# The first norm's squares taken from the transposed tiles of x, added by GpSimd and summed over partitions by TensorE

## The chip, the cores and the metric

The kernel runs on one core of a Trainium2 chip. The metric is the device time of one execution in microseconds, as the median of several runs. The engines are named as in the profile: PE (TensorE; PEld are its weight loads), DVE (VectorE), ACT (ScalarE), POOL (GpSimd) and SP (SyncE, which issues most DMA transfers). Each engine works through its own instructions in order; between engines, semaphores make an instruction wait.

## The reference

A trunk of two layers on x of 256 rows and 2048 columns, in float32. The change touches only the norm of the first layer and the projection that follows it:

```python
def rms_norm(x, g):
    xf = x.astype(jnp.float32)
    y = xf * lax.rsqrt(jnp.mean(xf * xf, axis=-1, keepdims=True) + EPS)
    return (y * g.astype(jnp.float32)).astype(x.dtype)

def gmlp_branch(xn, w_in, v_g, w_s, b_s, w_out):
    proj = xn @ w_in                              # [u | v | gate], each 4096 wide
    uv = jax.nn.gelu(proj[..., :2 * GMLP_WIDTH])
    zg = proj[..., 2 * GMLP_WIDTH:]
    u, v = jnp.split(uv, 2, axis=-1)
    v = rms_norm(v, v_g)
    ...

h = x
h = h + gmlp_branch(rms_norm(h, norm_g[0]), ...)
h = h + stick_breaking_branch(rms_norm(h, norm_g[1]), ...)
return rms_norm(h, final_g)
```

The norm's factor of a row of x, the reciprocal root of its mean square, is the same for all columns of the row. The kernel therefore multiplies x (times the gain) with the weights first, and applies the factor when it takes the products out of PSUM.

## The kernel before

All matmuls are done in float32 precision from two parts: an operand is rounded to a high part (`hi`, by ScalarE) and the rest is its low part (`lo`, by VectorE); a product is the sum of hi by hi, hi by lo and lo by hi, three matmuls of 128x512 each (`terms`). `cut` makes the parts of a tile of weights: a cast on ScalarE (L115), then a subtraction on VectorE (L116). `split_x` does the same for one contraction tile of x (128 columns of x, transposed: 128 partitions by 256 rows), with the gain: L479 on ScalarE, L480 on VectorE.

The first product is v's first two blocks of 512 columns, `v0`. Its first half of the contraction (tiles k = 0 to 7) runs over both blocks at once: for each k, 12 matmuls into four PSUM banks, with the weights `v_0` to `v_7` (`v_k_raw`, `v_k_hi`, `v_k_lo`) of 128x1024. The second half goes by columns: `v_08`, `v_010`, `v_012`, `v_014` hold two contraction tiles each of the first block, `v_18` and so on those of the second. The transposed x comes in `first` (tile 0) and `xr` (four tiles each), loaded by `load_x`. Beside this, x comes a second time, by rows: `load_h` loads four tiles `h` of 512 KB, and ScalarE squares each in two instructions with an accumulated sum (`square`, L474). `rstd` adds the sums (VectorE), and POOL raises the mean to the power -1/2 (`n_r`, L98). `evac_v` (L484) uses it.

From block 2 on, products of two blocks are computed with a Strassen-like scheme (`Pair`), which needs sums and differences of the parts of x: `left.sums` adds hi and lo (`s_full`), takes four differences (`s_sm`) and splits them again (`xs`). Before, these temporaries and the `h` tiles stand in buffers (tags `b11_1`, `b12_1`, `b21_1`, `b22_1`) that later hold weights `v_b` of the next pair; `v_p` are the parts of those weights.

The program's text doesn't fix the order in which engines get their work. A scheduler orders the instructions when the program is built, by its own model of their durations; `issue_after` and the order of the loads are bounds that it keeps. Weights' raw tiles rotate through four buffers, their parts through five. All loads of this stretch go through SP's queue in one order.

Of the kernel before, what the change touches and what calls it, by code (L numbers as in the profile page):

```python
# [29 lines left out]
def trunk_kernel(ctx: ExitStack, tc: tile.TileContext, x, xt, gcols, wst, wv0, a_w_in, a_v_norm_g,  # L30
# [19 lines left out]
    KD = D // P  # L50
    NC = D // CB
# [5 lines left out]
    const = ctx.enter_context(tc.tile_pool(name="const", bufs=1))  # L57
# [31 lines left out]
    def f(ap):  # L89
        return ap.bitcast(F32)  # L90

    def rstd(idx, nparts, n, name):
        tot = const.tile([P, NT], F32, name=f"{name}_tot")
        nc.vector.tensor_reduce(tot, ssq[:, :, idx, 0:nparts], axis=mybir.AxisListType.X, op=ALU.add)
        ms = const.tile([P, NT], F32, name=f"{name}_ms")
        nc.vector.tensor_scalar(ms, tot, 1.0 / n, EPS, op0=ALU.mult, op1=ALU.add)
        r = const.tile([P, NT], F32, name=f"{name}_r")
        nc.gpsimd.tensor_tensor(r, ms, half, op=ALU.pow)  # L98
        return r
# [7 lines left out]
    low = [None]  # L107
# [16 lines left out]
    class Left:  # L124
# [7 lines left out]
            sl = slice(t * P, (t + 1) * P)  # L132
            return self.hi[:, k, sl], self.lo[:, k, sl]

        def sums(self, ks, out, name):

            for k0 in range(0, ks, 4):
                n = min(4, ks - k0)
                full = []
                for i in range(2):  # L140
                    sl = slice(i * ks + k0, i * ks + k0 + n)
                    fl = sraw.tile([P, 4, S], F32, tag=f"b1{i + 1}_1", name=f"{name}_full{i}{k0}")
                    nc.vector.tensor_add(fl[:, 0:n], f(self.hi[:, sl, :]), f(self.lo[:, sl, :]))
                    full.append(fl)
                a11, a12 = full[0][:, 0:n, 0:P], full[1][:, 0:n, 0:P]
                a21, a22 = full[0][:, 0:n, P:S], full[1][:, 0:n, P:S]
                sm = [sraw.tile([P, 2, 4, P], F32, tag=f"b2{i + 1}_1", name=f"{name}_sm{i}{k0}") for i in range(2)]
                s1, s2, s3, s4 = sm[0][:, 0, 0:n], sm[0][:, 1, 0:n], sm[1][:, 0, 0:n], sm[1][:, 1, 0:n]
                nc.vector.tensor_sub(s1, a21, a22)
                nc.vector.tensor_sub(s3, a21, a11)  # L150
                nc.vector.tensor_sub(s2, a11, s1)
                nc.vector.tensor_sub(s4, a12, s2)
                for i, si in enumerate((s1, s2, s3, s4)):
                    o = out[:, :, i, k0:k0 + n]
                    nc.scalar.copy(o[:, 0], si)
                    nc.vector.tensor_sub(o[:, 1], si, f(o[:, 0]))
            self.s, self.ks = [out], ks
# [59 lines left out]
    def ins_of(x):  # L217
        return x.ins if hasattr(x, "ins") else x
# [219 lines left out]
    def home(tag, shape, dtype, name):  # L438
        return big.tile(shape, dtype, tag=tag, name=name)
# [4 lines left out]
    left = Left(x_hi, x_lo)  # L444
    vs_ = [home(f"v{i}", [P, NT, W // 2], F32, f"v{i}") for i in range(2)]

    def v_of(t, c0, n):

        i, c = divmod(c0, W // 2)
        return vs_[i][:, t, c:c + n]  # L450
    XC = 4
    raws = ("b11_0", "b12_0", "b22_0", "b21_0")
    xr = []

    def load_x(i):

        xr.append(sraw.tile([P, XC, S], F32, tag=raws[i], name=f"xr{i}"))
        if i > 0:
            load(xr[i], xt[:, i * XC:(i + 1) * XC, :])

    def x_of(k):
        return first[:, 0:S] if k == 0 else xr[k // XC][:, k % XC, :]

    hc = []

    def load_h(c):

# [14 lines left out]
    def evac_v(b, t, bank):  # L482
# [732 lines left out]
```

## Time and profile before

| | |
|---|---|
| median of 3 runs | 1142.49 us (1142.46 to 1146.1) |
| profiled execution: time, span | 1142.97 us, 1141.3 us |
| clock granted to TensorE | 0.999 of full speed |
| busy: PE, DVE, ACT, POOL | 1131.7, 1014.7, 832.5, 86.9 us |
| read from device memory, mean rate | 259.55 MB, 231 GB/s |

The span is from the first to the last instruction of the profiled execution, and its time includes what lies around it. Busy times are sums over the span. A matmul's end is modelled in this profile and overlaps the next, so the row's step from start to start (0.23 us for 128x512) says more than its duration.

### The profile page before, as it was taken

The page shows a single profiled execution, that of the slowest core. Times are in us where ns is not written, and L with a number is a line of the kernel's source. Part 1 is how long each engine was busy: PE and PEld are TensorE (multiplying, and loading weights), DVE is VectorE, ACT ScalarE, POOL GpSimd, SP SyncE. Part 2 cuts the span into 40 slices and gives each one's busy share as a digit, 9 for nine tenths or more (in the row PEclk, how much of TensorE's full clock was granted, in tenths as well). Part 3 has the DMA queues.
Part 4 walks back from the last instruction along what each step waited for, and adds up shares of the span by engine and source line. Part 5 has one row for each costly group of instructions (what it writes and reads, how often), then busy time and mean ns, then how long its engine had stood idle before and what let it go on. Part 6 is the DMA issues. An engine that isn't in the chain of part 4 may idle for free.

```text
span 1141.3 us, 14869 instructions
## 1 busy us (share of the span) xinstructions
PE 1131.7 (99%) x5169; PEld 937.7 (82%) x5169; DVE 1014.7 (89%) x1114; ACT 832.5 (73%) x1104; POOL 86.9 (8%) x106
## 2 busy tenths in 40 slices
PE   9999999999999999999999999999999999999997
PEld 6878888888888888888888888888888888888886
DVE  7999899999999999978989779889889989897986
ACT  7777678777777778766657457688678887886564
POOL 0210110110110110000010001100100101000000
PEclk9999999999999999999999999999999999999999
DMA  9997787687687687585785867687687776838951
GB/s 353 325 319 243 219 268 255 186 270 260 162 266 266 181 259 258 152 301 140 268 237 185 325 188 257 174 242 221 178 279 205 201 240 178 256 99 275 337 181 74
DMA packets 79227, 264.72 MB, mean 232 GB/s; under 512 B 9008, under 2 KB 9520, under 8 KB 79024
## 3 DMA queue, kind: packets, MB, share of 16 engines
q1 hardware_dynamic: 67472, 228.10, 57.0%
q0 software_dynamic: 10672, 33.04, 15.9%
q10 hardware_dynamic: 1008, 2.65, 0.6%
q8 instruction: 40, 0.66, 0.2%
q14 instruction: 35, 0.29, 0.1%
HBM read 259.55 MB, written 4.19 MB: 231 GB/s over the span
## 4 chain that ended last, share of the span: by engine, by line
PE 93%; DMA 3%; ACT 1%; DVE 1%; issue 1%; SPq 0%; DVEq 0%; POOLq 0%; POOL 0%; ACTq 0%
PE gu_a L120 3%; PE gu_b L120 3%; PE gu_a L121 3%; PE gu_b L121 3%; PE gu_b L122 3%; PE gu_a L122 3%; PE op_acc L122 2%; PE op_acc L120 2%; PE op_acc L121 2%; DMA v_raw<-in_a_w_in 2%; PE gu_d L120 2%; PE gu_d L121 2%; PE gu_c L120 2%; PE gu_c L122 2%; PE gu_d L122 2%; PE gu_c L121 2%
## 5 line engine op out<-in xcount | busy, mean ns | idle before, releaser
L115 ACT CAST gu_p_hi<-gu_b 128x1024 fp32r<-128x1024 f32 (+1 forms) x126 | 123.5, 1006 | 52.7 <-PE gu_c L122 17.7
L116 DVE TENSOR_TENSOR gu_p_lo<-gu_b,gu_p_hi 128x1024 fp32r<-128x1024 f32 (+1 forms) x126 | 143.5, 1164 | 10.0 <-ACT gu_p_hi L115 8.7
L116 DVE TENSOR_TENSOR qk_p_lo<-qk_b,qk_p_hi 128x1024 fp32r<-128x1024 f32 (+1 forms) x77 | 80.7, 1074 | 13.9 <-ACT qk_p_hi L115 13.3
L115 ACT CAST qk_p_hi<-qk_b 128x1024 fp32r<-128x1024 f32 (+1 forms) x77 | 70.5, 934 | 27.1 <-PE o_c L122 7.7
L115 ACT CAST gu_hi<-gu_raw 128x1024 fp32r<-128x1024 f32 x60 | 61.8, 1054 | 19.7 <-PE gu_d L122 13.5
L116 DVE TENSOR_TENSOR gu_lo<-gu_raw,gu_hi 128x1024 fp32r<-128x1024 f32 x60 | 71.4, 1216 | 4.8 <-ACT gu_hi L115 4.7
L116 DVE TENSOR_TENSOR v_p_lo<-v_b,v_p_hi 128x1024 fp32r<-128x1024 f32 x42 | 50.2, 1221 | 7.4 <-ACT v_p_hi L115 7.1
L115 ACT CAST v_hi<-v_raw 128x1024 fp32r<-128x1024 f32 (+1 forms) x43 | 41.9, 989 | 20.4 <-DMA v_raw<-in_a_w_in 9.8
L116 DVE TENSOR_TENSOR v_lo<-v_raw,v_hi 128x1024 fp32r<-128x1024 f32 (+1 forms) x43 | 49.1, 1146 | 7.2 <-ACT v_hi L115 6.8
L115 ACT CAST v_p_hi<-v_b 128x1024 fp32r<-128x1024 f32 x42 | 43.0, 1050 | 12.4 <-PE v_c L122 6.3
L116 DVE TENSOR_TENSOR bv_p_lo<-bv_b,bv_p_hi 128x1024 fp32r<-128x1024 f32 (+1 forms) x42 | 42.7, 1041 | 7.4 <-ACT bv_p_hi L115 7.1
L115 ACT CAST o_p_hi<-o_b 128x1024 fp32r<-128x1024 f32 (+1 forms) x35 | 33.4, 965 | 19.3 <-PE op_acc L122 13.8
L116 DVE TENSOR_TENSOR bg_p_lo<-bg_b,bg_p_hi 128x1024 fp32r<-128x1024 f32 (+1 forms) x42 | 42.5, 1042 | 5.0 <-ACT bg_p_hi L115 5.0
L115 ACT CAST bv_p_hi<-bv_b 128x1024 fp32r<-128x1024 f32 (+1 forms) x42 | 37.6, 908 | 12.8 <-PE qk_c L122 5.2
L115 ACT CAST bg_p_hi<-bg_b 128x1024 fp32r<-128x1024 f32 (+1 forms) x42 | 37.2, 906 | 9.4 <-PE bg_a L122 2.5
L116 DVE TENSOR_TENSOR o_p_lo<-o_b,o_p_hi 128x1024 fp32r<-128x1024 f32 (+1 forms) x35 | 38.2, 1113 | 5.3 <-ACT o_p_hi L115 5.3
L287 DVE TENSOR_TENSOR gu_b<-gu_b,gu_b 128x1024 f32<-128x1024 f32 (+1 forms) x36 | 41.5, 1165 | 1.1 <-DMA gu_b<-in_a_w_in 0.8
L115 ACT CAST op_hi<-op_raw 128x1024 fp32r<-128x1024 f32 x24 | 25.2, 1053 | 19.6 <-PE op_acc L122 10.8
L121 PE MATMUL op_acc<-op_lo,yc 128*128 128x512 f32 x96 | 37.7, 392 | 0.0
L122 PE MATMUL op_acc<-op_hi,yc 128*128 128x512 f32 x96 | 37.6, 394 | 0.0
L115 ACT CAST o_hi<-o_raw 128x1024 fp32r<-128x1024 f32 x22 | 23.0, 1055 | 19.9 <-PE o_d L122 10.2
L295 POOL DMA_DIRECT2D gu_b<-in_a_w_in x20 | 17.5, 874 | 251.0 <-DMA gu_raw<-in_a_w_in 79.5
(807 smaller groups left out, 3778.8 us busy)
## 6 DMA issues: line engine op xcount, KB each, us to landing
gu_b<-in_a_w_in SPq DMA_DIRECT2D x64, 512.0 KB, 4.9
gu_raw<-in_a_w_in SPq DMA_DIRECT2D x60, 512.0 KB, 5.2
v_raw<-in_a_w_in SPq DMA_DIRECT2D x32, 512.0 KB, 5.7
qk_b<-in_b_w_in SPq DMA_DIRECT2D x32, 512.0 KB, 4.7
qk_raw<-in_b_w_in SPq DMA_DIRECT2D x26, 512.0 KB, 5.2
v_b<-in_a_w_in SPq DMA_DIRECT2D x24, 512.0 KB, 5.1
op_raw<-in_a_w_out SPq DMA_DIRECT2D x24, 512.0 KB, 4.5
o_raw<-in_a_w_out SPq DMA_DIRECT2D x22, 512.0 KB, 4.7
```

The lines of the kernel that those rows point to most:

```text
L115: nc.scalar.copy(hi[:, sl], raw[:, sl])
L116: low[0] = nc.vector.tensor_sub(lo[:, sl], raw[:, sl], f(hi[:, sl]))
L120: nc.tensor.matmul(acc, lh, hi, start=first, stop=False, skip_group_check=True)
L121: nc.tensor.matmul(acc, lh, lo, start=False, stop=False, skip_group_check=True)
L122: nc.tensor.matmul(acc, ll, hi, start=False, stop=last, skip_group_check=True)
L287: nc.vector.tensor_sub(into[g], b0[g], b1[g])
L295: adds.append(nc.gpsimd.dma_start(into[g], self.src(HALVES[i][k], n, j), accum_op=ALU.add))
```

## The change

Each of the four groups of four contraction tiles of x (one of `first` and three of `xr0`, then `xr1`, `xr2`, `xr3`) is squared by ScalarE in whole (`square`), into a part of the tiles `vs_`, which are free that early (`slot`). POOL adds the four tiles of a group to one and that to a running total (`fold`: one add of 128x512 and one or two of 128x256). `rstd_x` splits the total into a high part (ScalarE) and a low part (VectorE), and four matmuls with a vector of ones sum over the partitions; then the mean and the power -1/2 follow as before. The four loads of x by rows and their squares are gone. `left.sums` gets its temporaries in `vs_` as well and is called earlier, bound to come after the low part of `v_08`. A power on POOL that nothing uses (`early`) is put at the start.

```diff
+    early = const.tile([P, NT], F32, name="early")
+    nc.gpsimd.tensor_tensor(early, nc.const_aps.tensor(1.0, [P, NT], F32), half, op=ALU.pow)
...
-        def sums(self, ks, out, name):
+        def sums(self, ks, out, name, at=None):
...
-                    fl = sraw.tile([P, 4, S], F32, tag=f"b1{i + 1}_1", name=f"{name}_full{i}{k0}")
+                    fl = sraw.tile([P, 4, S], F32, tag=f"b1{i + 1}_1", name=f"{name}_full{i}{k0}") if at is None else \
+                        at[i].rearrange("p (k s) -> p k s", k=4)
...
-    def load_h(c):
-        hc.append(sraw.tile([P, NT, CB], F32, tag=("b11_1", "b12_1", "b21_1", "b22_1")[c], name=f"h0_{c}"))
-        load(hc[c], x[c])
+    total = jk.tile([P, 2, S], F32, tag="sg0", bufs=1, name="total")
...
     def square(i):
-        c, t = divmod(i, NT)
-        junk = jk.tile([P, CB], BF16, tag="junk", bufs=1, name=f"junk0_{c}_{t}")
-        nc.scalar.activation(junk, hc[c][:, t, :], AF.Square, accum_out=ssq[:, t, 0, c:c + 1])
+        sq = slot(i).rearrange("p (k s) -> p k s", k=XC)
+        sqs.append(sq)
+        if i == 0:
+            nc.scalar.activation(sq[:, 0, :], first[:, 0:S], AF.Square)
+            nc.scalar.activation(sq[:, 1:XC, :], xr[0][:, 1:XC, :], AF.Square)
+        else:
+            nc.scalar.activation(sq, xr[i], AF.Square)
+
+    def fold(i):
+        sq = sqs[i]
+        nc.gpsimd.tensor_add(sq[:, 0:2], sq[:, 0:2], sq[:, 2:4])
+        nc.gpsimd.tensor_add(total[:, min(i, 1)], sq[:, 0], sq[:, 1])
+        if i > 0:
+            nc.gpsimd.tensor_add(total[:, 0], total[:, 0], total[:, 1])
+
+    def rstd_x():
+        parts = jk.tile([P, 2, S], F32R, tag="sg1", bufs=1, name="parts")
+        nc.scalar.copy(parts[:, 0], total[:, 0])
+        nc.vector.tensor_sub(parts[:, 1], total[:, 0], f(parts[:, 0]))
+        ones = const.tile([P, 2], F32R, name="ones_r")
+        nc.scalar.activation(ones, half, AF.Identity, scale=-2.0)
+        tot = ps_ms.tile([P, NT, 2], F32, tag="ms", name="n0_tot")
+        for t in range(NT):
+            for i in range(2):
+                nc.tensor.matmul(tot[:, t], parts[:, i, t * P:(t + 1) * P], ones, start=i == 0, stop=i == 1)
+        ms = const.tile([P, NT], F32, name="n0_ms")
+        nc.vector.tensor_scalar(ms, tot[:, :, 0], 1.0 / D, EPS, op0=ALU.mult, op1=ALU.add)
+        r = const.tile([P, NT], F32, name="n0_r")
+        nc.gpsimd.tensor_tensor(r, ms, half, op=ALU.pow)
+        return r
...
-    beyond = {3: lambda: load_x(1), 4: lambda: load_x(2), 5: lambda: load_h(0), 6: lambda: load_x(3),
-              7: lambda: load_h(1)}
+    beyond = {3: lambda: load_x(1), 4: lambda: load_x(2), 6: lambda: load_x(3)}
...
-        if k >= 6:
-            square(k - 6)
+        if k in (4, 6, 7, 9):
+            square((4, 6, 7, 9).index(k))
+        if k in (4, 6, 7, 9):
+            fold((4, 6, 7, 9).index(k))
...
-            r1 = rstd(0, NC, D, "n0")
+            r1 = rstd_x()
         next(col)
-        if i < 2:
-            load_h(2 + i)
-        if i < 3:
-            square(2 + 2 * i)
-            square(3 + 2 * i)
-    left.sums(KS_A, home("xs", [P, 2, 4, KS_A, P], F32R, "xs0"), "s0")
+        if i == 0:
+            with tc.issue_after(ins_of(low[0])):
+                left.sums(KS_A, home("xs", [P, 2, 4, KS_A, P], F32R, "xs0"), "s0",
+                          [slot(i) for i in (4, 5, 0, 1)])
+        if KD // 2 + i in (4, 6, 7, 9):
+            square((4, 6, 7, 9).index(KD // 2 + i))
+        if KD // 2 + i in (4, 6, 7, 9):
+            fold((4, 6, 7, 9).index(KD // 2 + i))
```

The scheduler puts the new work among the old as follows; behind the first pair of blocks the order of every engine is the same as before. Numbers in names are the program's own.

On ScalarE, before, from the scaling of x's tile 3 to the cast of `v_6` (`xr_195` and `xr_217` hold x's tiles 4 to 7 and 8 to 11, `h_0` rows of x):

```order
L479 ACTIVATE x_hi<-xr_122,cols 128x256
L115 CAST v_3_hi<-v_3_raw 128x1024
L479 ACTIVATE x_hi<-xr_195,cols 128x256 x4
L115 CAST v_4_hi<-v_4_raw 128x1024
L479 ACTIVATE x_hi<-xr_217,cols 128x256 x4
L115 CAST v_5_hi<-v_5_raw 128x1024
L474 ACTIVATE junk_0_0_269,ssq<-h_0_239 128x512
L474 ACTIVATE junk_0_1_293,ssq<-h_0_239 128x512
L115 CAST v_6_hi<-v_6_raw 128x1024
```

On ScalarE now, the same stretch (`v_117` and `v_118` are the tiles `vs_` with the squares):

```order
L483 ACTIVATE v_117<-xr_125 128x768
L117 CAST v_3_hi<-v_3_raw 128x1024
L514 ACTIVATE x_hi<-xr_198,cols 128x256 x3
L485 ACTIVATE v_117<-xr_198 128x1024
L514 ACTIVATE x_hi<-xr_198,cols 128x256
L117 CAST v_4_hi<-v_4_raw 128x1024
L485 ACTIVATE v_118<-xr_220 128x1024
L514 ACTIVATE x_hi<-xr_220,cols 128x256 x4
L117 CAST v_5_hi<-v_5_raw 128x1024
L117 CAST v_6_hi<-v_6_raw 128x1024
```

The squares of the first three groups stand ahead of `v_3_hi`, `v_4_hi` and `v_5_hi`; before, the first square stood behind `v_5_hi`.

On VectorE, before, the products' low parts from `v_6` on and the sums (`s_full`, `s_sm`):

```order
L143 TENSOR_TENSOR s_full_430<-x_hi,x_lo 128x1024
L116 TENSOR_TENSOR v_6_lo<-v_6_raw,v_6_hi 128x1024
L480 SCALAR_TENSOR_TENSOR x_lo<-xr_261,cols,x_hi 128x256 x4
L116 TENSOR_TENSOR v_7_lo<-v_7_raw,v_7_hi 128x1024
L143 TENSOR_TENSOR s_full_432<-x_hi,x_lo 128x1024
L116 TENSOR_TENSOR v_08_lo<-v_08_raw,v_08_hi 128x1024
```

On VectorE now, from `v_6` on (`v_118<-x_hi,x_lo` are the two sums that were `s_full`):

```order
L118 TENSOR_TENSOR v_6_lo<-v_6_raw,v_6_hi 128x1024
L515 SCALAR_TENSOR_TENSOR x_lo<-xr_266,cols,x_hi 128x256 x4
L118 TENSOR_TENSOR v_7_lo<-v_7_raw,v_7_hi 128x1024
L118 TENSOR_TENSOR v_08_lo<-v_08_raw,v_08_hi 128x1024
L146 TENSOR_TENSOR v_118<-x_hi,x_lo 128x1024 x2
L118 TENSOR_TENSOR v_010_lo<-v_010_raw,v_010_hi 128x1024
L498 TENSOR_TENSOR parts<-total,parts 128x256
```

The two sums moved from ahead of `v_6_lo` and `v_08_lo` to behind `v_08_lo`, and the low part of the total follows `v_010_lo`.

On TensorE now, the first of the four matmuls over the partitions (`n_tot`) between the products of `v_08` (before, the row didn't exist and the others stood in the same order):

```order
L122 MATMUL v_acc_120<-v_08_hi,x_hi 128x512
L122 MATMUL v_acc_121<-v_08_hi,x_hi 128x512
L504 MATMUL n_tot<-ones_r,parts 128x2
L123 MATMUL v_acc_120<-v_08_lo,x_hi 128x512
L124 MATMUL v_acc_120<-v_08_hi,x_lo 128x512
L123 MATMUL v_acc_121<-v_08_lo,x_hi 128x512
```

It stands ahead of all products of `v_08` with its low part; the other three come behind the first two products of `v_012`.

More of the change, by code (lines that the diff above doesn't have):

```diff
@@ L146, in sums @@
                 a21, a22 = full[0][:, 0:n, P:S], full[1][:, 0:n, P:S]
-                sm = [sraw.tile([P, 2, 4, P], F32, tag=f"b2{i + 1}_1", name=f"{name}_sm{i}{k0}") for i in range(2)]
+                sm = [sraw.tile([P, 2, 4, P], F32, tag=f"b2{i + 1}_1", name=f"{name}_sm{i}{k0}") if at is None else
+                      at[2 + i].rearrange("p (h k s) -> p h k s", h=2, k=4) for i in range(2)]
                 s1, s2, s3, s4 = sm[0][:, 0, 0:n], sm[0][:, 1, 0:n], sm[1][:, 0, 0:n], sm[1][:, 1, 0:n]
@@ L450, in v_of, with slot @@
         return vs_[i][:, t, c:c + n]
+    def slot(i):
+        v, t, c = ((0, 0, 1), (0, 1, 1), (1, 0, 0), (1, 0, 1), (1, 1, 0), (1, 1, 1))[i]
+        n = NT * CB
+        return vs_[v][:, t, c * n:(c + 1) * n]
     XC = 4
@@ L462, in x_of @@
         return first[:, 0:S] if k == 0 else xr[k // XC][:, k % XC, :]
-    hc = []
-    def load_h(c):
-        hc.append(sraw.tile([P, NT, CB], F32, tag=("b11_1", "b12_1", "b21_1", "b22_1")[c], name=f"h0_{c}"))
-        load(hc[c], x[c])
+    total = jk.tile([P, 2, S], F32, tag="sg0", bufs=1, name="total")
+    sqs = []
     def square(i):
-        c, t = divmod(i, NT)
-        junk = jk.tile([P, CB], BF16, tag="junk", bufs=1, name=f"junk0_{c}_{t}")
-        nc.scalar.activation(junk, hc[c][:, t, :], AF.Square, accum_out=ssq[:, t, 0, c:c + 1])
+        sq = slot(i).rearrange("p (k s) -> p k s", k=XC)
[26 more added lines that the diff above has]
+        return r
     def split_x(k):
```

## The prediction

> **What bounds the kernel now.** I read the page's head first, then the list of what TensorE waited for, then the engines' busy time in the stretch that the change touches (10 to 30 us), and then that stretch instruction by instruction. In the waits the columns are total, times, longest; in the stretches, busy us (instructions) of PE, PEld, DVE, ACT and POOL, then clock, DMA share and GB/s.
>
> ```profile
> span 1141.3 us, 14869 instructions
> PE 1131.7 (99%) x5169; PEld 937.7 (82%) x5169; DVE 1014.7 (89%) x1114; ACT 832.5 (73%) x1104; POOL 86.9 (8%) x106
> ...
> PE wps L78 <- PEq L1203: 0.8, 1, 0.8
> PE v_acc L120 <- ACT v_hi L115: 0.8, 1, 0.8
> PE v_c L120 <- ACT v_c L332: 0.4, 1, 0.4
> PE gT L435 <- ACT bsg L1024: 0.2, 1, 0.2
> ...
> 10.00:15.00 5.00, 5.00 (x24) 4.08 (x23) 4.11 (x8) 4.16 (x8) 0.00 (x0) 1.00 1.03 408
> 15.00:20.00 5.00, 5.00 (x24) 4.14 (x23) 4.92 (x9) 4.97 (x12) 0.00 (x0) 1.00 1.03 415
> 20.00:25.00 5.00, 5.00 (x24) 4.14 (x23) 5.00 (x8) 4.83 (x10) 0.00 (x0) 1.00 1.02 408
> 25.00:30.00 5.00, 5.00 (x24) 4.14 (x23) 4.67 (x6) 4.81 (x11) 0.00 (x0) 1.00 1.03 407
> ```
>
> TensorE is the bound: it works in 99% of the span, and after the first matmuls its waits add up to 1.4 us in the whole run. So little is to be gained anywhere, and each microsecond by which TensorE is made to wait at the start is added to the end, since no later idle time absorbs it. From 10 to 30 us VectorE, ScalarE and the DMA engines are all full as well and TensorE just keeps its pace (clock 1.00); POOL does nothing there. The question is by how much the new work of ScalarE and POOL makes VectorE late in that stretch. The rows below are ScalarE's, VectorE's and one weight load of TensorE's (start, duration; a group xN counts as one).
>
> ```profile
> 11.62 0.51 ACT L479 ACTIVATE x_hi<-xr,cols 128x256 fp32r<-128x256 f32 x1
> 12.16 1.05 ACT L115 CAST v_hi<-v_raw 128x1024 fp32r<-128x1024 f32 x1
> 13.45 1.72 ACT L479 ACTIVATE x_hi<-xr,cols 128x256 fp32r<-128x256 f32 x4 [0.24 <-DMA xr<-in_xt]
> 15.06 1.03 ACT L115 CAST v_hi<-v_raw 128x1024 fp32r<-128x1024 f32 x1
> 16.01 1.71 ACT L479 ACTIVATE x_hi<-xr,cols 128x256 fp32r<-128x256 f32 x4
> 17.62 1.04 ACT L115 CAST v_hi<-v_raw 128x1024 fp32r<-128x1024 f32 x1
> ...
> 13.24 1.23 DVE L116 TENSOR_TENSOR v_lo<-v_raw,v_hi 128x1024 fp32r<-128x1024 f32 x1 [0.33 <-ACT v_hi L115]
> 14.38 1.67 DVE L480 SCALAR_TENSOR_TENSOR x_lo<-xr,cols,x_hi 128x256 fp32r<-128x256 f32 x4
> 16.13 1.23 DVE L116 TENSOR_TENSOR v_lo<-v_raw,v_hi 128x1024 fp32r<-128x1024 f32 x1
> 17.27 1.67 DVE L480 SCALAR_TENSOR_TENSOR x_lo<-xr,cols,x_hi 128x256 fp32r<-128x256 f32 x4
> 18.86 1.22 DVE L116 TENSOR_TENSOR v_lo<-v_raw,v_hi 128x1024 fp32r<-128x1024 f32 x1
> 20.08 1.23 DVE L143 TENSOR_TENSOR s_full<-x_hi,x_lo 128x1024 f32<-128x1024 f32 x1
> ...
> 20.88 0.19 PEld L121 LDWEIGHTS v_acc<-v_lo,x_hi 128*128 128x128 f32 x1
> 28.58 0.19 PEld L121 LDWEIGHTS v_acc<-v_lo,x_hi 128*128 128x128 f32 x1
> ```
>
> The last three L115 rows are v_3_hi, v_4_hi and v_5_hi, the L116 rows v_3_lo, v_4_lo and v_5_lo. TensorE takes up v_5_lo at 20.88, 0.8 us after it is done (18.86 + 1.22 = 20.08): that is all the room there is. From start to next start, a 128x1024 cast takes ScalarE 0.95 us (15.06 to 16.01), four 128x256 scalings 1.61 (13.45 to 15.06; 0.40 each), and VectorE needs 1.14 for a low part (13.24 to 14.38) and 1.59 for four x_lo (17.27 to 18.86).
>
> **The change, part 1: ScalarE's squares come before the casts that TensorE needs.** The change puts a 128x768 square ahead of v_3_hi and a 128x1024 square ahead of each of v_4_hi and v_5_hi; before, no square stood ahead of v_5_hi. No row has a 128x1024 square; the nearest is the cast of that size, 0.95, and I take 0.74 for 768. From 11.62: 0.40 + 0.74 + 0.95 (v_3_hi) + 1.61 + 0.95 + 0.95 (v_4_hi) + 0.95 + 1.61 = 8.16, so v_5_hi starts at 19.78 instead of 17.62 and ends at 20.82; v_5_lo ends 1.22 later, at 22.04. By ScalarE alone TensorE is 1.2 us late. Were these squares free (lower bound), 0. Of the loads, v_3 to v_5 and their x tiles stand ahead of the first removed load in SP's queue, so they come no earlier.
>
> **Part 2: POOL's adds hold VectorE up.** POOL had nothing here. Its reads are priced by the row in which POOL meets a busy VectorE:
>
> ```profile
> 253.69 1.22 DVE L116 TENSOR_TENSOR gu_lo<-gu_raw,gu_hi 128x1024 fp32r<-128x1024 f32 x1
> 254.83 1.43 DVE L315 TENSOR_TENSOR gu_b<-gu_b,gu_b 128x1024 f32<-128x1024 f32 x1
> ...
> 254.16 1.01 POOL L615 TENSOR_SCALAR_AFFINE_SELECT ws<-ws 128x256 f32<-128x256 f32 x1 [6.95 <-DMA ws<-in_wst]
> 424.85 2.76 POOL L615 TENSOR_SCALAR_AFFINE_SELECT ws<-ws 128x256 f32<-128x256 f32 x1 [4.67 <-DMA ws<-in_wst]
> L615 POOL TENSOR_SCALAR_AFFINE_SELECT ws<-ws 128x256 f32<-128x256 f32 x8 | 9.4, 1173 | 45.8 <-DMA ws<-in_wst 45.8
> ```
>
> The select starts at 254.16, while VectorE is busy; it ends at 255.17, 0.34 after VectorE's next instruction began, and that instruction takes 1.43 instead of 1.22. So POOL waits for a gap between two VectorE instructions, and its reading of 256 elements a partition then costs VectorE 0.21. An add with two inputs of 512 reads 1024, one of 256 reads 512. Folds 0 to 2 (one add of 128x512 and one of 128x256, then twice one and two) read 3 x 1024 + 5 x 512 = 22 x 256 elements: 22 x 0.21 = 4.62 us. Their squares are done by about 12.9, 15.9 and 18.2, so all of it falls ahead of the end of v_5_lo. VectorE's own way there, from v_3_lo (12.76 + 1.04, thus 13.83): 1.14 + 1.59 + 1.14 + 1.59 + 1.22 = 6.68, to 20.51; with the holds 25.13. TensorE wants it at 20.88: **4.25 us late**. ScalarE's 22.04 is inside that, so parts 1 and 2 make 4.25 together and not 5.4. Ends: if POOL holds nothing up, 1.2 (part 1); if VectorE is shut out for the whole 0.34 per 256, 22 x 0.34 = 7.5, to 28.0, thus 7.1 late. I take 0.21, since it is what the row shows for a read.
>
> [...]
>
> Behind v_5_lo the sums' two 128x1024 adds (1.14 each) now stand after v_08_lo, which frees 2.28 before it, and fold 3 takes 8 x 0.21 = 1.7 of that: nothing more. The late x loads are no help, since VectorE is the late one.
>
> **Part 3: four matmuls of 128x2.** They stand in TensorE's order between v_08's and v_012's.
>
> ```profile
> 698.45 1.03 PE L435 MATMUL hT<-ident,h 128*128 128x128 f32 x8
> 699.24 0.48 PE L120 MATMUL qk_c<-qk_p_hi,xs 128*128 128x512 f32 x1
> ...
> 60.55 0.63 ACT L486 ACTIVATE junkv<-v 128x512 bf16<-128x512 f32 x1
> 61.17 0.58 ACT L332 COPY v_c<-v_b 128x512 f32<-128x512 f32 x1
> ...
> 33.02 5.09 POOL L98 TENSOR_TENSOR n_r<-n_ms,half 128x2 f32<-128x2 f32 x1 [31.64 <-DVE n_ms L96]
> 184.40 0.73 POOL L98 TENSOR_TENSOR nv_r<-nv_ms,half 128x2 f32<-128x2 f32 x1 [9.11 <-DVE nv_ms L96]
> 39.06 1.26 ACT L484 ACTIVATE v<-v_acc,n_r 128x512 f32<-128x512 f32 x2
> ...
> 3.29 0.51 ACT L479 ACTIVATE x_hi<-first,cols 128x256 fp32r<-128x256 f32 x1 [0.54 <-DMA cols<-in_gcols]
> 4.39 1.28 ACT L115 CAST v_hi<-v_raw 128x512 fp32r<-128x512 f32 x2 [0.60 <-DMA v_raw<-in_wv]
> h<-in_x SPq DMA_DIRECT2D x8, 512.0 KB, 8.2
> ```
>
> The nearest are transposes, 0.79 / 8 = 0.1 each: **+0.4** (0 to 0.8). The first waits for ScalarE's copy of POOL's total and stands where TensorE is at 28.58 now, 32.8 when 4.25 late. POOL's last squares are ready at about 22.7 (two more casts and one square after 19.78); three adds with a wait each end near 27. Six microseconds of room: 0. If it is gone, v_08's low products and all behind them wait there.
>
> **Part 4: the rest.** The copy v_c has two squares of `junkv` ahead of it now and one in the changed order; that is 0.6 us of ScalarE, and TensorE's only wait in this stretch (0.4 at v_c) goes: **-0.4** (0 to -0.6). Nothing is late next there, as no other wait is listed. The four removed loads are 512 KB each, at 408 GB/s 1.28 us, 5.1 us of DMA time; all stand behind v_5's load, at a time when VectorE and not the DMA sets the pace, and TensorE had no wait for a load after 10 us: 0. The `early` power moves the long first one (5.09 against 0.73) to the start, where POOL is idle until 12.9, and before its end at 38.11 was covered by ScalarE's first use at 39.06: 0. The constant of ones and the first square (0.2 and 0.4) are covered by ScalarE's idle 0.54 and 0.60 at 3.29 and 4.39; without that cover they would cost 0.6. VectorE's added `parts` (0.40) and removed reduction (0.15) fall in its freed time.
>
> Sum: 4.25 + 0.4 - 0.4 = +4.25 on the profiled execution, 1142.97 us by its own time (span 1141.3 and 1.7 around it). It stands 0.5 above the median of the three runs, 1142.49, from which I count: **1146.7 us**.
>
> **The rivals.**
> 1. Not slower: POOL's adds cost VectorE nothing, or POOL alone waits. For it: the select itself waited up to 2.76 us and VectorE lost only 0.21. Then part 1 remains: 1142.5 + 1.2 = 1143.7, within what a measurement of this kernel can tell from no change (0.3%, 3.4 us). It decides where the delay is 3.4 us, v_5_lo then ending at 24.3: 3.8 us of holds, or 0.17 per 256 elements read.
> 2. Longer holds: POOL's two-input adds keep VectorE out for their whole time. For it: 0.34 from grant to end; against it: only 0.21 showed on VectorE. 7.1 + 0 = 1149.6.
> 3. POOL's chain comes too late for TensorE's n_tot. Eleven adds start at 12.9; the mean of the small selects is 1.17 with one input of 256. At 2 us each they end at 34.9, the copy at 35.4, 6.8 after 28.58: 1149.3. It decides from about 1.8 us an add when VectorE is 4.25 late.
> 4. The saved DMA time pays: 0.4 of TensorE's waits goes and the squares hide behind earlier loads: 1142.1. Against it: v_3 to v_5 aren't loaded earlier.
>
> **How the numbers follow.** The forecast (POOL's reads delay VectorE by about 0.21 per 256) has 0.50, with 1145.3 to 1148.3 as its own range; a sixth of it (0.08) lies below 1145.9, within 0.3%. Rival 1 has 0.28, rivals 2 and 3 together 0.19, rival 4 0.03. Slower by over 0.3%: 0.42 + 0.19 = 0.61; within: 0.08 + 0.28 + 0.02 = 0.38; faster by over 0.3%: 0.01, as TensorE's waits hold less than that. The range goes from rival 1 with 0.4 off (1143.3) to rival 2 (1149.7).
>
> **What would show it.** In the changed profile: v_5_lo ending near 25 instead of 20.08; VectorE's instructions between 13 and 25 us longer by 0.4 to 0.9 where a POOL add runs; a new wait of TensorE for v_4_lo and v_5_lo of about 4 us in all, none at n_tot; no wait at v_c; everything behind 90 us as before but later. Wrong if v_5_lo ends near 22 (rival 1), beyond 27 (rival 2), or if TensorE's wait stands at n_tot (rival 3).

## The result and the profile after

The changed kernel takes 1149.86 us (median of 6 runs, 1148.67 to 1150.26) against 1142.93 us for the kernel before on the same chip (6 runs, 1141.75 to 1146.1): ratio 1.0058, 95% interval 1.0047 to 1.0069, thus 6.9 us slower. The profiled execution took 1150.13 us. From here on times are those of the profile's span, and the page's head and TensorE's waits (total, times, longest) answer to the first rows shown of before:

```profile
span 1148.4 us, 14872 instructions
PE 1136.0 (99%) x5173; PEld 939.8 (82%) x5173; DVE 1021.0 (89%) x1114; ACT 831.0 (72%) x1095; POOL 101.8 (9%) x118
...
PE v_acc L123 <- DVE v_lo L118: 3.3, 2, 3.1
...
PE v_c L122 <- ACT v_c L336: 0.4, 1, 0.4
```

TensorE now waits 3.3 us for low parts that VectorE makes, where it waited for none. The 0.8 of `v_hi` at 9.59 us in the old profile is gone (v's second tile had landed 1.26 us sooner); such waits at the start differ between runs (none here, 0.5 in the run without the adds). The wait at `v_c` has stayed.

The engines' busy time in the stretch that the change touches, columns as before (PE, PEld, DVE, ACT, POOL, then clock, DMA share, GB/s):

```profile
10.00:15.00 5.00, 5.00 (x23) 3.83 (x21) 3.21 (x6) 4.70 (x9) 2.25 (x2) 1.00 1.02 414
15.00:20.00 5.00, 3.21 (x13) 2.10 (x12) 5.00 (x6) 5.00 (x9) 4.74 (x5) 1.00 0.85 342
20.00:25.00 5.00, 3.62 (x9) 2.84 (x10) 5.00 (x5) 4.95 (x8) 4.76 (x5) 0.52 0.34 107
25.00:30.00 5.00, 4.76 (x18) 3.36 (x17) 5.00 (x8) 1.05 (x1) 0.89 (x2) 0.80 0.32 111
```

From 20 to 25 us VectorE is busy throughout but finishes 5 instructions instead of 8; POOL is busy beside it. TensorE, which issued 24, issues 9, and for part of the time at half clock (0.52 on the mean). The DMA falls to a third: raw weights wait for the buffers that VectorE is late to free (SP's longest wait for a `v_lo` from 15 to 30 us is 5.9 us, before it was 2.3). Now VectorE's and POOL's instructions there (start, duration):

```profile
13.56 1.49 DVE L118 TENSOR_TENSOR v_lo<-v_raw,v_hi 128x1024 fp32r<-128x1024 f32 x1 [0.92 <-ACT v_hi L117]
14.98 4.14 DVE L515 SCALAR_TENSOR_TENSOR x_lo<-xr,cols,x_hi 128x256 fp32r<-128x256 f32 x4
19.05 2.28 DVE L118 TENSOR_TENSOR v_lo<-v_raw,v_hi 128x1024 fp32r<-128x1024 f32 x1
21.25 4.12 DVE L515 SCALAR_TENSOR_TENSOR x_lo<-xr,cols,x_hi 128x256 fp32r<-128x256 f32 x4
25.30 2.89 DVE L118 TENSOR_TENSOR v_lo<-v_raw,v_hi 128x1024 fp32r<-128x1024 f32 x2
...
12.68 1.30 POOL L489 TENSOR_TENSOR v<-v 128x512 f32<-128x512 f32 x1 [10.67 <-ACT v L483]
14.05 1.61 POOL L490 TENSOR_TENSOR total<-v 128x256 f32<-128x256 f32 x1
...
18.80 1.44 POOL L489 TENSOR_TENSOR v<-v 128x512 f32<-128x512 f32 x1
20.32 1.60 POOL L490 TENSOR_TENSOR total<-v 128x256 f32<-128x256 f32 x1
...
22.75 1.46 POOL L489 TENSOR_TENSOR v<-v 128x512 f32<-128x512 f32 x1
...
25.18 0.79 POOL L492 TENSOR_TENSOR total<-total 128x256 f32<-128x256 f32 x1
```

The first three `v_lo` rows are `v_3_lo`, `v_4_lo` and, in the pair at 25.30, `v_5_lo` (1.75 of the 2.89, so it ends at 27.05). Four `x_lo` take 4.14 and 4.12 instead of 1.67, the two single low parts 0.26 and 1.05 more than 1.23, `v_5_lo` 0.53 more: 6.8 us in all. POOL and VectorE take turns, one instruction each: eleven adds make eleven instructions of VectorE longer. Taken apart by the steps of single instructions, an add of 128x512 costs VectorE 1.04 us and one of 128x256 0.48, that is 0.24 to 0.26 per 256 elements read. All eleven adds, the last fold's three (22.75 to 25.97) among them, lie ahead of the end of `v_5_lo`.

Where the 6.9 us arise is seen by counting TensorE's 128x512 products and comparing the start of the n-th one with that of the old profile (the ten warm-up products in bfloat16 are left out, and the count starts at 0). The columns are five places: the 20th product (11.1 us before; all runs are 0.6 to 1.3 early there, since the old profile has its 0.8 at `v_hi`), the 68th (22.0, four behind `v_5_lo`), the 152nd (41.1, behind the four matmuls `n_tot`), the 212th (54.7, behind the first blocks' evacuation) and the 284th (71.9, behind `v_c`; from there the difference is constant). The rows of the runs below stand in the same table; us later than in the old profile. Each row is of one profiled execution, the ratio of the median: the profile of the adds alone took 0.9 us more than its median and that of the adds on VectorE 1.0 less, the others are within 0.5:

| kernel | 20 | 68 | 152 | 212 | 284 | ratio of the times |
|---|---|---|---|---|---|---|
| changed | -0.8 | +6.1 | +6.7 | +7.0 | +6.9 | 1.0058 |
| no adds | -0.7 | +0.4 | +0.9 | +2.5 | +1.9 | 1.0020 |
| adds alone | -1.0 | +5.7 | +6.0 | +6.0 | +7.2 | 1.0056 |
| copies | -0.9 | +0.6 | +1.1 | +2.9 | +3.1 | 1.0027 |
| kept busy | -0.7 | +5.9 | +6.4 | +6.8 | +6.0 | 1.0050 |
| adds on VectorE | -0.6 | +0.5 | +1.0 | +2.9 | +2.0 | 1.0032 |
| sums alone | -0.9 | -0.9 | -0.3 | +2.1 | +1.2 | 1.0022 |
| last fold later | -1.3 | +4.4 | +4.9 | +6.7 | +6.2 | 1.0070 |
| product for power | -0.6 | +6.1 | +6.7 | +6.7 | +6.3 | 1.0063 |
| sums, n_r on VectorE | -1.0 | -1.0 | +0.1 | +0.1 | -0.3 | 0.9999 |
| last fold, n_r on VectorE | -1.0 | +5.1 | +5.6 | +5.6 | +4.7 | 1.0049 |
| all on VectorE | -0.7 | +1.4 | +2.1 | +2.1 | +1.1 | 1.0014 |
| wide add ahead | -0.8 | +5.6 | +6.1 | +6.9 | +6.8 | 1.0066 |

In the changed kernel 6.9 come up to `v_5_lo` (-0.8 to +6.1), 0.5 at `n_tot` and 0.3 at the evacuation; the 0.8 of the start comes off. Kernels that are the same up to the 68th product differ there by 0.5 (changed, product for power, wide add) to 0.7 us (the two with the last fold later).

### The profile page after: what moved, and what is told of

Read it like the earlier page. It is cut to its first block, busy times and chain, and to the rows that moved or that the text cites. A ratio compares the mean times of both kernels' runs of the same rounds, so it can differ in the third digit from the quotient of the medians.

```text
span 1148.4 us, 14872 instructions
## 1 busy us (share of the span) xinstructions
PE 1136.0 (99%) x5173; PEld 939.8 (82%) x5173; DVE 1021.0 (89%) x1114; ACT 831.0 (72%) x1095; POOL 101.8 (9%) x118
## 4 chain that ended last, share of the span: by engine, by line
PE 96%; ACT 1%; issue 1%; DVE 1%; DMA 1%; SPq 0%; DVEq 0%; POOLq 0%; POOL 0%; ACTq 0%
PE gu_a L123 3%; PE gu_b L123 3%; PE gu_a L122 3%; PE gu_b L122 3%; PE gu_a L124 3%; PE gu_b L124 3%; PE op_acc L124 2%; PE op_acc L122 2%; PE op_acc L123 2%; PE gu_d L123 2%; PE gu_c L123 2%; PE gu_d L122 2%; PE gu_c L122 2%; PE gu_d L124 2%; PE gu_c L124 2%; PE qk_a L124 1%
## 5 line engine op out<-in xcount | busy, mean ns | idle before, releaser
L117 ACT CAST v_hi<-v_raw 128x1024 fp32r<-128x1024 f32 (+1 forms) x43 | 41.9, 990 | 23.9 <-DMA v_raw<-in_a_w_in 12.0
```

Source lines behind the costliest of these rows:

```text
L117: nc.scalar.copy(hi[:, sl], raw[:, sl])
```

## The experiments

The theory was that POOL's two-input adds hold VectorE up. Its rivals: that ScalarE's squares ahead of the casts do it; that the half clock of TensorE costs the time itself; and for the long `n_r`, that it is the power's own. Each run was timed beside the kernel before on the same chip, and its ratio is to that.

**No adds**

```diff
-        nc.gpsimd.tensor_add(sq[:, 0:2], sq[:, 0:2], sq[:, 2:4])
-        nc.gpsimd.tensor_add(total[:, min(i, 1)], sq[:, 0], sq[:, 1])
-        if i > 0:
-            nc.gpsimd.tensor_add(total[:, 0], total[:, 0], total[:, 1])
+        if i == 3:
+            nc.gpsimd.tensor_add(total[:, 0], sq[:, 0], sq[:, 1])
```

> The changed kernel with ten of the eleven POOL adds left out (only the last one of 128x256 stays, so the norm is of a part of the squares and the output differs); all squares, the four matmuls and the sums in v's tiles stay. If POOL's adds hold VectorE up (about 0.25 us per 256 elements read), v_5_lo ends near 22.0 by ScalarE's squares alone, TensorE is some 1.2 us late there, with 0.4 for the four matmuls about 1144.5 us, within 0.3% of before. If it is ScalarE's squares ahead of the casts that make the low parts late, nothing changes: v_5_lo near 27 and 1149.9. If the long n_r power (6.84 us) is caused by the adds ahead of it on POOL, it is near 0.7 here; if VectorE's back-to-back work starves it, it stays at 5 to 7.

Measured: 1145.39 us, ratio 1.0020 (1.0011 to 1.0029). VectorE's rows, and POOL's power:

```profile
16.63 1.23 DVE L118 TENSOR_TENSOR v_lo<-v_raw,v_hi 128x1024 fp32r<-128x1024 f32 x1 [0.46 <-ACT v_hi L117]
17.98 1.69 DVE L513 SCALAR_TENSOR_TENSOR x_lo<-xr,cols,x_hi 128x256 fp32r<-128x256 f32 x4
20.12 2.36 DVE L118 TENSOR_TENSOR v_lo<-v_raw,v_hi 128x1024 fp32r<-128x1024 f32 x2 [0.45 <-ACT v_hi L117]
...
32.55 12.05 POOL L506 TENSOR_TENSOR n_r<-n_ms,half 128x2 f32<-128x2 f32 x1 [9.48 <-DVE n_ms L504]
```

Every instruction of VectorE up to `v_5_lo` has its old length again, VectorE now waits for ScalarE (0.46, 0.45), and `v_5_lo` ends at 21.35. TensorE is 1.1 us late there (-0.7 to +0.4), as the squares alone were said to cost. So the adds make the delay. The time came out 0.9 above the 1144.5 expected, and the table shows where: +0.9 to +2.5 at the evacuation, where `n_r` ends only at 44.60. With almost no adds on POOL it took 12.05 us: what is long about it isn't the adds.

**Adds alone**, put into the kernel before:

```diff
...
+    def fold(i):
+        sq = slot(i).rearrange("p (k s) -> p k s", k=XC)
+        nc.gpsimd.tensor_add(sq[:, 0:2], xr[i][:, 1:3], xr[i][:, 2:4])
+        nc.gpsimd.tensor_add(total[:, min(i, 1)], sq[:, 0], sq[:, 1])
+        if i > 0:
+            nc.gpsimd.tensor_add(total[:, 0], total[:, 0], total[:, 1])
...
+        if k in (4, 6, 7):
+            fold((4, 6, 7).index(k))
...
+        if i == 1:
+            fold(3)
```

> The kernel before with the eleven POOL adds alone put in (they read x's tiles and write free slots of v that nothing reads; no squares of ScalarE are moved, the norm is computed as before). If POOL's adds hold VectorE up, the 22 units of folds 0 to 2 at 0.25 make v_5_lo 5.5 us later (25.6) and TensorE 4.7 late, and fold 3 adds its 2.0 while VectorE is still full: 1147.6 to 1149.7. If ScalarE's squares are the cause, no change: 1142.9, v_5_lo at 20.1.

Measured: 1149.40 us, ratio 1.0056 (1.0043 to 1.0068). TensorE's waits and VectorE's rows:

```profile
PE v_acc L121 <- DVE v_lo L116: 5.3, 4, 2.2
PE v_c L120 <- ACT v_c L332: 1.9, 1, 1.9
...
16.62 4.15 DVE L494 SCALAR_TENSOR_TENSOR x_lo<-xr,cols,x_hi 128x256 fp32r<-128x256 f32 x4
...
21.82 3.67 DVE L494 SCALAR_TENSOR_TENSOR x_lo<-xr,cols,x_hi 128x256 fp32r<-128x256 f32 x4
25.42 1.21 DVE L116 TENSOR_TENSOR v_lo<-v_raw,v_hi 128x1024 fp32r<-128x1024 f32 x1
```

With no square moved, the adds alone cost as much as the whole change, and VectorE's rows are longer in the same way. They cost 6.7 up to `v_5_lo` (-1.0 to +5.7) in four short waits; `v_5_lo` ended at 26.6, 1.0 later than expected, since the last fold ran ahead of it here too (VectorE has 30 units to bear, not 22). Another 1.2 came at `v_c`.

**Copies** in place of the adds, with one input:

```diff
-        nc.gpsimd.tensor_add(sq[:, 0:2], sq[:, 0:2], sq[:, 2:4])
-        nc.gpsimd.tensor_add(total[:, min(i, 1)], sq[:, 0], sq[:, 1])
+        nc.gpsimd.tensor_copy(sq[:, 0:2], sq[:, 2:4])
+        nc.gpsimd.tensor_copy(total[:, min(i, 1)], sq[:, 1])
...
-            nc.gpsimd.tensor_add(total[:, 0], total[:, 0], total[:, 1])
+            nc.gpsimd.tensor_copy(total[:, 0], total[:, 1])
```

> The changed kernel with POOL copies (one input) in place of the eleven adds (two inputs), so that POOL reads half of the elements; the norm is then of a part of the squares and the output differs. If a hold goes with the elements that POOL reads (0.25 us per 256): 15 units, 3.4 to 3.75 us of holds, v_5_lo at 23.9 to 24.3 and 1146.5. If it goes with the number of POOL instructions, 1149.9 and v_5_lo at 27. If only two-input instructions of POOL hold VectorE up, 1144.5 and v_5_lo at 22.

Measured: 1146.43 us, ratio 1.0027 (1.0017 to 1.0037), just what the elements read would give. But the reason isn't that, as VectorE's rows show:

```profile
14.44 2.02 DVE L515 SCALAR_TENSOR_TENSOR x_lo<-xr,cols,x_hi 128x256 fp32r<-128x256 f32 x4
16.77 1.23 DVE L118 TENSOR_TENSOR v_lo<-v_raw,v_hi 128x1024 fp32r<-128x1024 f32 x1 [0.31 <-ACT v_hi L117]
18.13 2.09 DVE L515 SCALAR_TENSOR_TENSOR x_lo<-xr,cols,x_hi 128x256 fp32r<-128x256 f32 x4
20.27 2.36 DVE L118 TENSOR_TENSOR v_lo<-v_raw,v_hi 128x1024 fp32r<-128x1024 f32 x2
```

The two groups of `x_lo` are only 0.35 and 0.42 longer, VectorE still waits for ScalarE in between, and `v_5_lo` ends at 21.5 instead of 23.9 or later. A copy holds VectorE up far less than half of what an add does: about 0.14 us for each one ahead of `v_5_lo`, of 512 or of 256. The other 2.5 us came behind `v_5_lo` (+0.6 to +3.1), mostly at the evacuation, where `n_r` took 6.78. The total alone would have confirmed a false price.

**Kept busy**: twelve idle matmuls behind the high products of tiles 4 and 5.

```diff
...
+                    warm = ps_ms.tile([P, CB], F32, tag="ms", name=f"warm{k}")
+                    with tc.issue_after(ins_of(hh)):
+                        for _ in range(12):
+                            hh = nc.tensor.matmul(warm, ones[:, 0:P], ones, start=True, stop=True)
...
```

(The lines left out issue the products of these two tiles in their old order around it.)

> The changed kernel with twelve idle matmuls (into an unused bank) behind the high products of each of the pairs of rows 4 and 5, so that TensorE does not idle while it waits for v_4_lo and v_5_lo. If TensorE only waits for VectorE (v_5_lo at 27.05), the half clock between 20 and 27 us costs at most 0.3: the granted clock is 1.0 there and the time 1149.6 to 1150.2. If the half clock is what costs, the 2.4 us that the products ran longer come back: 1147.4.

Measured: 1149.27 us, ratio 1.0050 (1.0036 to 1.0064); the changed kernel has 1.0058 (1.0047 to 1.0069). The clock is the third column from the end:

```profile
20.00:25.00 5.00, 4.52 (x21) 2.78 (x19) 5.00 (x5) 4.73 (x8) 4.69 (x6) 1.00 0.36 106
25.00:30.00 5.00, 4.93 (x23) 3.19 (x21) 5.00 (x8) 1.04 (x1) 0.74 (x1) 1.00 0.37 122
```

The clock is full, and up to `v_5_lo` TensorE is as late as ever (+5.9 against +6.1). The products ran 2.4 us longer at half clock in time in which they would have waited anyway. The total lies between the two expectations, nearer to the first; the 0.6 that it is below the changed kernel is within the intervals, and most of it arises at `v_c`.

**Adds on VectorE** (`nc.vector.tensor_add` in the three lines of `fold`).

> The changed kernel with the eleven adds on VectorE itself instead of POOL. From VectorE's rows (1.14 us for 128x1024, so about 0.58 for 128x512 and 0.30 for 128x256) they cost it 4 x 0.58 + 7 x 0.30 = 4.4 us. If POOL's adds hold VectorE up by 0.25 us per 256 elements read (7.5 us), the same sums are cheaper on VectorE: 3.0 us less, near 1147. If VectorE loses only what POOL's reads need and the rest of the delay has another cause, it is no faster than the changed kernel: 1149.9 or more.

Measured: 1146.34 us, ratio 1.0032 (1.0019 to 1.0045). VectorE does the eleven adds itself in 0.60 and 0.34 from start to start, 4.8 us together, against the 6.8 for which POOL held it up to `v_5_lo`. TensorE is 1.1 late at `v_5_lo` (-0.6 to +0.5) instead of 6.9; 1.9 more come at the evacuation, behind an `n_r` of 5.63 us.

**Last fold later**, behind the cast of tiles 8 and 9:

```diff
+            with tc.issue_after(ins_of(high[0])):
+                square(3)
+            fold(3)
```

(`high[0]` is the last cast; the fold's old place is taken out.)

> The changed kernel with the last square and its three adds put behind the cast of rows 8 and 9 (about 26 us) instead of behind that of row 6, so that they run after v_5_lo; the four matmuls come later by it. If the prediction's step was wrong only in where this fold fell (it ran ahead of v_5_lo) and VectorE has the freed 2.28 us behind it, v_5_lo ends near 25.1 and the time is 2.0 us less, 1147.9. If VectorE has no room there after all, the 2.0 us only move on to the next low parts: 1149.9.

Measured: 1150.03 us, ratio 1.0070 (1.0057 to 1.0083): no gain. VectorE's row of `v_5_lo` and `v_6_lo`, TensorE's first product with `v_5_lo`, and the last fold and `n_r` on POOL:

```profile
23.43 2.35 DVE L118 TENSOR_TENSOR v_lo<-v_raw,v_hi 128x1024 fp32r<-128x1024 f32 x2
...
25.27 0.57 PE L123 MATMUL v_acc<-v_lo,x_hi 128*128 128x512 f32 x1
...
26.68 1.43 POOL L489 TENSOR_TENSOR v<-v 128x512 f32<-128x512 f32 x1 [4.25 <-ACT v L485]
...
47.82 5.64 POOL L508 TENSOR_TENSOR n_r<-n_ms,half 128x2 f32<-128x2 f32 x1 [2.27 <-DVE n_ms L506]
```

`v_5_lo` ends 2.4 us sooner (24.6 against 27.05) and TensorE is 1.7 less late at the 68th product; 0.6 of that is from the start, and 0.6 of what VectorE won is lost to TensorE, which comes to `v_5_lo` only at 25.27 (last section). From there to the 152nd product the delay grows no more than in the changed kernel (by 0.5 in both): VectorE does have room for this fold behind `v_5_lo`. The gain was given back at the evacuation (+4.9 to +6.7), since `n_tot` and with it `n_r` came later.

**Sums alone** in the kernel before: the `at=` of `sums` and its call at `i == 0`.

> The kernel before with one part of the change alone: the sums and their temporaries in v's tiles, behind the low part of rows 8 and 9; the squares of x's rows and their loads stay. If that move frees VectorE's 2.28 us in the stretch of 20 to 22.5 us and nothing else, TensorE's waits there are already nil: 1142.9, same as before within 0.1%. If the moved sums are themselves part of the cost (they come late for the fifth products, or collide at 32 us), it is slower by 0.5 or more.

Measured: 1144.50 us, ratio 1.0022 (1.0013 to 1.0032): slower, the second of the two. Up to the 68th product it is level with the start (-0.9 in both columns); 2.4 come at the evacuation (-0.3 to +2.1). The rows there are TensorE's longest wait, POOL's power, and VectorE's around its end:

```profile
PE v_acc L120 <- ACT v_hi L115: 1.5, 1, 1.5
...
32.69 9.70 POOL L98 TENSOR_TENSOR n_r<-n_ms,half 128x2 f32<-128x2 f32 x1 [31.32 <-DVE n_ms L96]
...
40.60 1.21 DVE L116 TENSOR_TENSOR v_p_lo<-v_b,v_p_hi 128x1024 fp32r<-128x1024 f32 x1
41.85 1.23 DVE L289 TENSOR_TENSOR v_b<-v_b,v_b 128x1024 f32<-128x1024 f32 x1
```

The power started at 32.69, as early as before, but ended at 42.39 instead of 38.11, 0.58 after the end of the first row. VectorE worked without a gap from `n_ms` to 41.81; then comes one of 0.04.

**Product for power**: `op=ALU.mult` in `n_r`.

> The changed kernel with a product in place of the power n_r (the scale of the norm and the output differ). If POOL's long instruction n_r (6.84 us) is shut out by VectorE's back-to-back work, the product of 128x2 takes 5 to 7 us as well, ends just as VectorE first pauses, and the time stays at 1149.9. If it is the power's own first use, it takes under 1 us, and the time is 0.3 less.

Measured: 1149.41 us, ratio 1.0063 (1.0050 to 1.0075). The product took as long as the power, nearly:

```profile
42.86 6.32 POOL L508 TENSOR_TENSOR n_r<-n_ms,half 128x2 f32<-128x2 f32 x1 [16.92 <-DVE n_ms L506]
```

**`n_r` on VectorE**, as a product, in three kernels: sums alone, last fold later, and adds on VectorE.

```diff
-        nc.gpsimd.tensor_tensor(r, ms, half, op=ALU.pow)
+        nc.vector.tensor_tensor(r, ms, half, op=ALU.mult)
```

(In the first kernel, whose `rstd` serves other norms too, for this norm alone.)

> The kernel before with the sums moved (as in the run of the sums alone, 1144.5), and n_r as a product on VectorE in place of POOL's power (the norm's scale and so the output differ). If the moved sums cost time because POOL's n_r is shut out until VectorE pauses (9.70 us, to 42.34, and ScalarE, and TensorE behind it, wait for it: 1.53 at 46.03), that wait goes and the time is some 2 us less, 1142.5. If the moved sums cost time by themselves, it stays at 1144.5.

> The changed kernel with the last fold later (1150.03) and n_r as a product on VectorE (the output differs). If the 1.75 us that the later fold won up to v_5_lo were given back because n_r came too late for ScalarE's evacuation (n_r ended at 53.46, TensorE waited 1.28 at 54.23), that wait goes: 1148.5. If something else gives them back, 1150.0.

> The changed kernel with the eleven adds on VectorE (1146.34) and n_r as a product there too (the output differs), so that POOL does no arithmetic in this part. If the rest of the cost was POOL's n_r being shut out (TensorE waited 1.44 at 50.51), 1.4 to 1.9 less: 1144.4 to 1144.9. If not, 1146.3.

Measured: 1142.64 (ratio 0.9999, 0.9989 to 1.0008), 1148.44 (1.0049, 1.0036 to 1.0061) and 1144.22 us (1.0014, 1.0005 to 1.0022): each 1.6 to 2.1 us below its pair (2.1 to 2.6 by the ratios). In the first of them

```profile
35.28 0.15 DVE L99 TENSOR_TENSOR n_r<-n_ms,half 128x2 f32<-128x2 f32 x1
```

takes 0.15 us, and in all three TensorE has no wait at the evacuation (from the 152nd to the 212th product +2.4, +1.8 and +1.9 become 0.0, 0.0 and 0.0). So the moved sums cost nothing in the total once `n_r` is off POOL. With the last fold later the gain at `v_5_lo` is now kept: 1148.44 is 1.4 us below the changed kernel, though the intervals of the two ratios overlap. No version beats the kernel before: the first is level with it and the third still slower.

**A wide add ahead of `n_r`**:

```diff
...
+        nc.gpsimd.tensor_add(wide, total[:, 1], total[:, 1])
...
```

(The mean, `n_ms`, is written into `total[:, 1]`, so that the add waits for it.)

> The changed kernel with one more POOL add, of 128x256, that waits for n_ms and stands directly ahead of n_r; nothing reads it. If POOL is shut out of a run of VectorE's two-input instructions whatever it does, this add takes the 5 to 7 us that n_r took and n_r ends at the same time or 0.7 later: 1149.9 to 1150.5. If only the small size of n_r (128x2) keeps it out, the wide add gets in after one VectorE instruction and ends within 2 us, holding VectorE up by 0.5; n_r still waits behind it.

Measured: 1150.04 us, ratio 1.0066 (1.0053 to 1.0079). POOL's rows, and VectorE's last one before its pause:

```profile
42.20 6.74 POOL L508 TENSOR_TENSOR wide<-total 128x256 f32<-128x256 f32 x1 [16.91 <-DVE total L506]
48.90 0.70 POOL L510 TENSOR_TENSOR n_r<-total,half 128x2 f32<-128x2 f32 x1
...
47.25 1.20 DVE L291 TENSOR_TENSOR v_b<-v_b,v_b 128x1024 f32<-128x1024 f32 x1
```

The wide add waits as `n_r` did, to 0.5 us after VectorE's last instruction, and the power behind it, with VectorE idle, takes 0.70. Neither the power nor the small size makes it long.

## Why the prediction was right, and where it was not

The direction, the mechanism and the place were right: POOL's adds hold VectorE up, TensorE gets `v_4_lo` and `v_5_lo` late, and nothing later takes the time back. The size was off: the changed kernel lost 6.9 us where 4.25 were forecast. Counted from the prediction's 1142.49 by the ratio it takes 1149.1, inside the range up to 1149.7 but beyond the forecast's own range, which ended at 1148.3; that the whole range holds it is owed to the second rival's end and not to the sum. The 1148.3 was an estimate, a delay of 5.8 us (1148.3 less 1142.5), and no run shows the price of POOL's adds in it; the runs showed 1.04 and 0.48 us an add, and in the changed kernel a delay of 6.9 at `v_5_lo` (-0.8 to +6.1).

- **Part 1**, ScalarE's squares: 1.2 by themselves, hidden behind VectorE's own delay. Without the adds TensorE was 1.1 late.
- **Part 2** is the mis-sized term: 4.25 against 6.9. Two of its steps failed. The price, 0.21 per 256 elements, came from a select with one input; the adds cost 0.24 to 0.26. And the last fold was put behind `v_5_lo`; it ran ahead of it, since its square came at 21.4 and VectorE, late by the other adds, reached `v_5_lo` only at 25.30. The prediction's own times say as much: the squares ready at about 22.7, and `v_5_lo` begun at 23.9 (25.13 less 1.22). 22 units at 0.25 instead of 0.21 are 0.9 us more and the last fold's 8 units 2.0, together 2.9 where 2.7 were missing. That a fold behind `v_5_lo` costs nothing more was right, as the later fold showed (+0.5 from the 68th to the 152nd product, as in the changed kernel). `v_5_lo` ended at 27.05; the text had set "beyond 27" as the mark of the second rival, longer holds. That rival's total, 1149.6, is nearly the measured one, but by other factors: 22 units at 0.34, where it was 30 at 0.25.
- **Part 3**, four matmuls: 0.4 forecast. The steps of the products around them (34.72 to 35.29 and 40.32 to 41.11 us, two steps of 0.23 each taken off) leave 0.45. The table's +0.5 alone would not show it, since the sums alone lose 0.6 between the same places without these matmuls. TensorE didn't wait for the total at `n_tot`; the room was enough.
- **Part 4**: the `v_c` wait didn't go (0.4 in both profiles). ScalarE did reach `v_c` 0.6 sooner behind the evacuation ahead of it (64.39 to 68.05 us instead of 56.89 to 61.17), but that evacuation began 7.5 later, 0.5 more than TensorE's own delay of 7.0. The wait does go in several of the runs above, and what decides it was not settled. The removed loads gave nothing that shows (the DMA share is 0.34 and 0.32 from 20 to 30 us), though no run leaves them out alone. `early` was to shorten `n_r`; it took 0.70 itself and `n_r` took 6.84 (5.09 before). The step took the 5.09 for the cost of a first use. It was the wait for a pause of VectorE, and the move of the sums made that later. "Covered" was nearly right for the changed kernel (0.3 us), because TensorE was late already; where TensorE was less late, the same wait cost 1.6 to 2.4 (no adds, copies, adds on VectorE, sums alone: 152nd to 212th product).
- **Rivals**: the first (1143.7) had its own mechanism right, but the adds did cost. The third (POOL's chain late at `n_tot`) didn't come about: on POOL an add took 0.8 to 1.6 us, and the chain ended at 25.97. The fourth fell: the DMA had time to spare (a share of 0.34 and 0.32 from 20 to 30 us).

## What to carry to other kernels

Work that is put on POOL because POOL is idle isn't free where VectorE is the engine that sets the pace: here its two-input adds held VectorE up for longer than VectorE needs to do them itself (6.8 against 4.8 us). A short POOL instruction on a critical chain, such as this norm's power, may end only when VectorE next pauses (5.09 to 12.05 us here, 0.70 with VectorE idle), so ask which instructions of VectorE stand behind its input, and make it early or put it on another engine. When an experiment gives the expected total, look at the place too: the run with copies hit its number for another reason.

## What the hardware showed that I had not expected

A POOL instruction can be shut out by VectorE for as long as VectorE works without a pause, up to 11.5 us here (no adds, 32.55 to 44.03). The power started as soon as its input was there and ended 0.57 or 0.58 us after VectorE's first pause in all of these:

| kernel | start | duration | VectorE's work ends | end |
|---|---|---|---|---|
| before | 33.02 | 5.09 | 37.53 | 38.11 |
| changed | 42.88 | 6.84 | 49.14 | 49.72 |
| no adds | 32.55 | 12.05 | 44.03 | 44.60 |
| adds alone | 39.00 | 5.09 | 43.51 | 44.09 |
| sums alone | 32.69 | 9.70 | 41.81 | 42.39 |

For the changed kernel in rows (POOL's power, VectorE's last instruction before the pause and the next one, ScalarE's evacuation that waited):

```profile
42.88 6.84 POOL L508 TENSOR_TENSOR n_r<-n_ms,half 128x2 f32<-128x2 f32 x1 [16.91 <-DVE n_ms L506]
...
47.93 1.21 DVE L291 TENSOR_TENSOR v_b<-v_b,v_b 128x1024 f32<-128x1024 f32 x1
51.98 1.23 DVE L118 TENSOR_TENSOR v_p_lo<-v_b,v_p_hi 128x1024 fp32r<-128x1024 f32 x1 [2.84 <-ACT v_p_hi L117]
...
49.75 1.27 ACT L519 ACTIVATE v<-v_acc,n_r 128x512 f32<-128x512 f32 x2 [5.04 <-POOL n_r L508]
```

VectorE's own instructions are not longer there (1.21 us for 128x1024, 1.23 behind the pause). Between 13 and 26 us, on the other hand, the adds got in behind nearly every instruction of VectorE. What decides between the two is open; the runs rule out the operation (the product took 6.32), the size of the instruction (the wide add 6.74) and the adds ahead of it (12.05 with one add left). Two low parts in a row don't keep POOL out either: with the last fold later two adds of 128x256 got in there (3.43 us for the pair at 28.32 instead of 2.35). One difference was not varied: whatever was shut out had been released by VectorE itself (`n_ms`), the adds by ScalarE or by POOL's own add before them.

The wait of TensorE brought its clock down (0.52 from 20 to 25 us, against 1.00 in the run kept busy). The products behind the wait step by 0.43 us from start to start, those at the end by 0.23:

```profile
17.09 1.19 PE L122 MATMUL v_acc<-v_hi,x_hi 128*128 128x512 f32 x4
21.38 0.79 PE L123 MATMUL v_acc<-v_lo,x_hi 128*128 128x512 f32 x1 [3.10 <-DVE v_lo L118]
...
24.54 0.63 PE L124 MATMUL v_acc<-v_hi,x_lo 128*128 128x512 f32 x1
24.96 1.91 PE L122 MATMUL v_acc<-v_hi,x_hi 128*128 128x512 f32 x4
27.10 0.50 PE L123 MATMUL v_acc<-v_lo,x_hi 128*128 128x512 f32 x1 [0.23 <-DVE v_lo L118]
27.44 0.40 PE L124 MATMUL v_acc<-v_hi,x_lo 128*128 128x512 f32 x1
```

From about 18.0 (17.09 + 4 x 0.23) to 21.38, 3.4 us, TensorE began no product. The granted clock fell within that wait: narrower stretches of the same view have 1.00 up to 20.0, 0.70 from 20.0 to 20.5 and 0.50 from there to 27.0. Taken from the start of the last product before the wait to that of the first behind it, 3.35 to 3.51 us, such a fall came in all five runs that have so long a step (changed, product for power, wide add, and the two with the last fold later), whose mean granted clock is 0.995 to 0.997; the longest step of the adds alone, 2.58 us, brought none (0.998). The fall stood at no fixed distance from the last product: it came 2.3 us behind its start here (at about 20.2), and 4.7 with the last fold later (at about 22.2), when TensorE was already back at work. In the changed kernel the next wait covered the slow steps; with the last fold later it did not: `v_5_lo` was ready at 24.6 and TensorE, at half clock since about 22, took it at 25.27.
